# Attention in a two-layer hybrid model: K in one padded tile per head, and projection units taken as their buffers come free

## The chip, the cores and the metric

One core of a Trainium2 chip runs the whole inference step as one program. The metric is the device time of one execution in microseconds (us). The engines are TensorE (PE, with its weight loads shown as PEld), VectorE (DVE), ScalarE (ACT), GpSimd (POOL) and SyncE (SP, which issues DMA transfers). Each engine works through its own instructions in order.

## What is computed

The model has a state-space layer and an attention layer, each followed by a feed-forward layer; 1024 new prompt rows and 64 sample rows (continuing an older stream) are processed, 1088 in all, 1024 wide. The change is in the attention layer only. Cut to what matters:

```
K, V = split(rmsnorm(x) @ w_kv)                 # 16 heads of 64, K and V shared, also outputs
q    = rmsnorm(x) @ w_q
# prompt: queries in chunks of 64, each sees its own chunk and the 8 before
# sample: 64 queries see 512 cached keys and 64 new ones
s = q k^T * 64**-0.5 + rel_bias[clip(qpos - kpos, -256, 256) + 256]
s = where(valid, s, -inf);  p = softmax(s);  o = p v;  mixer = o @ w_o
```

## The kernel before

Projections run in three slices of columns (rows of x): `SL` = 0 to 383, 384 to 767, 768 to 1087; the last 64 columns of slice 2 are the sample. Heads are taken in eight pairs. For each pair and slice there is one projection **unit** for each of K, V and Q: nine units a pair. A unit is 24 matmuls (`mm`, lines 454 to 456: eight steps of depth, three passes that give float32 precision from split operands), 384 or 320 columns wide. It is issued in four parts of six matmuls, and between the parts TensorE takes other work from a list of tasks.

Attention of a pair runs in nine **blocks** of 128 queries; block 8 is the sample with 64. A block has three stages:

- **Scores.** For each head, K times the high and the low part of Q into a PSUM tile `S` (lines 1692 and 1693), then VectorE adds the bias and takes the extreme (1702), ScalarE takes the exponential (1707), and VectorE the reciprocal and the scaling (1708, 1709). A block sees up to five tiles of 128 keys, 640 columns.
- **Transposes.** TensorE transposes the probabilities (`ptp`, 1724), VectorE (first head) and ScalarE (second head) copy them out (1729, and 1731 for the last 64 rows of block 8).
- **Values.** Probabilities times V (`po`, 1763), three blocks at once when the first block of the next slice has had its transposes.

`S` and `ptp` share two PSUM buffers; the projections have two of their own. Each of K's tiles holds one slice of one head in `[high; low]` halves (`evk`, lines 1586 to 1603, with two ScalarE casts 1598 and two VectorE subtractions 1599), so that the scores of a block are cut wherever its keys cross a slice: block 6 needs three pieces of 128, 384 and 128 columns for each head. `evq` (1605 to 1625) does the same for Q with four casts; `evv` (1637) hands V to a task that transposes it (`vtp`, 1632, copied at 1634). `load_bias` brings each head's bias by DMA and has POOL clear its two corners (1578, 1579); there are three such buffers for two heads a pair. The weights of later units are prepared by ScalarE and VectorE (`hl`, lines 350 and 353).

The order on TensorE is written by the program: it runs a modelled clock `st.t` and picks tasks by it. The orders on the other engines are found by a scheduler with priorities when the program is built. The units of a pair come in a fixed order, K V Q of slice 0, then of slice 1, then of slice 2; before each the loop waits until the buffers it writes are free, and meanwhile other tasks run:

```
for s, i in [(s, i) for s in range(NSL) for i in range(3) if j > 1 or s == 2 or i == 2]:
    q = 3 * j + s
    if (s, i) == (2, 0):
        st.spawn(side_task(j))
    st.wait_for(lambda: cur["A"] >= 3 * (q - 1) if i == 2 else free_q(q, "AC"[i]))
    units(ws[i], j, evs[i], (s,))
```

`cur["A"]` counts the blocks whose scores are issued. `V`, `A`, `G` and `PE` stand for the four engines, `P` is 128, `T` 1088, `WIN` 640.

Of the kernel before, what the change touches and what calls it, by code (L numbers as in the profile page):

```python
# [374 lines left out]
def hybrid_kernel(  # L375
# [1165 lines left out]
    with ExitStack() as es:  # L1541
# [5 lines left out]
        pos = {}  # L1547

        def load_pair(j):
            kqv[j] = dict(K={}, Q={}, V={})  # L1550

        def load_side(j):
            d = kqv[j]
# [26 lines left out]
                bias.append(bt)  # L1580
            kqv[j]["bias"] = bias

        def k_tiles():
            return [sb2.tile([P, 384], F32R, tag=f"K{e}", bufs=KBUF, name=f"K{e}") for e in range(2)]

        def evk(j):
            d = kqv[j]

            def f(s, p_):
                n = SL[s][1]  # L1590
                st.wait_for(lambda: ("rb", s) in done)
                kf = sb2.tile([P, 384], F32, tag="kqv", bufs=2, name="kf")
                with tc.high_priority(HIP):
                    V.tensor_tensor(kf[:, :n], p_[:, :n], rba[s][:, :n], op=ALU.mult)
                Kd = d["K"].get(s) or k_tiles()
                for e in range(2):
# [3 lines left out]
                d["K"][s] = Kd  # L1600
                if s:
                    a_, b_, c_ = (128, 384, 0) if s == 1 else (0, 320, 256)
                    nc.sync.dma_start(kT_o[j * P:(j + 1) * P, c_:c_ + b_ - a_], kf[:, a_:b_])
            return f

        def evq(j):
            def f(s, p_):
                n = SL[s][1]

                Q = [[sb2.tile([P, 384], F32R, tag=f"Q{x}{e}", bufs=2, name=f"Q{x}{e}") for x in "hl"] for e in range(2)]  # L1610
                kqv[j]["Q"][s] = Q
                qf = sb2.tile([P, 384], F32, tag="kqv", bufs=2, name="qf")
                with tc.high_priority(HIP):
                    V.scalar_tensor_tensor(qf[:, :n], p_[:, :n], 0.125, rba[s][:, :n], op0=ALU.mult, op1=ALU.mult)
                for e in range(2):
                    qh, ql = Q[e]
                    A.copy(qh[H2[e], :n], qf[H2[e], :n])
# [9 lines left out]
        def v_task(j, s, vt):  # L1627
            Vn = kqv[j]["V"][s] = sb2.tile([P, 3, P], F32, tag="Vn", bufs=KBUF, name="Vn")
            pt = ax("vtp")
            for i in range(3):  # L1630
                L = CHL[3 * s + i]
                PE.transpose(pt[:L, i * P:(i + 1) * P], vt[:, i * P:i * P + L], ident)
            nf = 3 if s < 2 else 2
            V.tensor_copy(Vn[:, :nf, :], pt[:, :nf * P].rearrange("p (a b) -> p a b", b=P))
            if s == 2:
                V.tensor_copy(Vn[:64, 2, :], pt[:64, 256:384])
# [18 lines left out]
        def att_task(j, b):  # L1655
# [6 lines left out]
            )  # L1662
            L = CHL[b]

            pcs_ = []
# [11 lines left out]
            parts, bank, fill = [], 0, 0  # L1677
            for kd_, ko, fw in pcs_:
                if fill + fw > 512:
                    bank, fill = bank + 1, 0  # L1680
                parts.append((bank, fill, kd_, ko, fw))
                fill += fw
            split = sum(p_[4] for p_ in parts if p_[0] == 0)
            nkt = (w_ + P - 1) // P
            sts = []
            for e in range(2):
                sp = psS.tile([P, 2, 512], F32, tag="S", name="S")
                qs = slice(i * P, i * P + L)
                qh, ql = d["Q"][s][e]
                for bank, f0, kd_, ko, fw in parts:  # L1690
                    dst = sp[:L, bank, f0:f0 + fw]
                    PE.matmul(dst, qh[:, qs], kd_[e][:, ko:ko + fw], start=True, stop=False)
                    PE.matmul(dst, ql[:, qs], kd_[e][:, ko:ko + fw], start=False, stop=True)
# [3 lines left out]
                brev = bt[:L, 0:w_][:, ::-1] if b < 8 else bt[:L, 64:640][:, ::-1]  # L1697

                low = TOP
                with tc.high_priority(ATP):  # L1700
                    for pi, (f0, f1) in enumerate([(0, split)] + ([(split, w_)] if split < w_ else [])):
                        V.tensor_tensor_reduce(  # L1702
                            out=sc[:L, f0:f1], in0=sp[:L, pi, :f1 - f0], in1=brev[:, f0:f1],
                            scale=-1.0, scalar=low, op0=ALU.add, op1=ALU.min, accum_out=mx[:L, pi:pi + 1],
                        )
                        low = mx[:L, pi:pi + 1]
                    A.activation(sc[:L, :w_], sc[:L, :w_], AF.Exp, bias=low, scale=-1.0, accum_out=mx[:L, 3:4])
                    V.reciprocal(mx[:L, 3:4], mx[:L, 3:4])
                    V.tensor_scalar(sc[:L, :w_], sc[:L, :w_], mx[:L, 3:4], None, op0=ALU.mult)
# [9 lines left out]
            for e in range(2):  # L1719
                pT = late["sb3"].tile([P, 5, P], F32, tag="pT", bufs=6, name="pT")  # L1720
                pt = psS.tile([P, 2, 512], F32, tag="S", name="ptp").rearrange("p a b -> p (a b)")
                for kt in range(nkt):
                    kw = min(P, w_ - kt * P)
                    PE.transpose(pt[:kw, kt * P:kt * P + L], sts[e][:L, kt * P:kt * P + kw], ident[:L, :L])  # L1724
                ptv = pt[:, :640].rearrange("p (a b) -> p a b", b=P)
                nfull = w_ // P
                cpf = A.copy if e else V.tensor_copy
                with tc.high_priority(ATP):
                    cpf(pT[:, :nfull, :L], ptv[:, :nfull, :L])
                    if nfull < nkt:  # L1730
                        cpf(pT[:64, nfull, :L], ptv[:64, nfull, :L])
                PTs.append(pT)
            cur["B"] = seqn + 1
            cost += 1.1 * w_ / 640
# [10 lines left out]
        def values(blocks):  # L1745

            cost = 0
            while blocks:
# [3 lines left out]
                    pos["po"] = ax("po")  # L1752
                po = pos["po"]
                for kt in range(nkt):
                    kw = min(P, w_ - kt * P)
                    for e in range(2):
                        if 3 * s + i < 8:
                            vs = d["V"][(k0 + kt) // 3][:, (k0 + kt) % 3, 64 * e:64 * e + 64]
                        elif kt < 4:
                            vs = d["Cv"][:, kt, 64 * e:64 * e + 64]  # L1760
                        else:
                            vs = d["V"][2][:64, 2, 64 * e:64 * e + 64]
                        PE.matmul(  # L1763
                            po[64 * e:64 * e + 64, i * P:i * P + L], vs, PTs[e][:kw, kt, :L],
                            start=(kt == 0), stop=(kt == nkt - 1),
                        )
                if i == 2:
# [57 lines left out]
                if s and w is wv:  # L1825
                    W.put()

        kqv[0]["K"][2] = k_tiles()
        units(W.get(), 1, evk, (0, 1))
        W.put()  # L1830
        st.wait_for(lambda: 2 in done)
# [25 lines left out]
        for j in range(1, 8):  # L1857
# [3 lines left out]
            ws = [W.get(), W.get() if j > 1 else wv, W.get()]  # L1861
            evs = [evk, evv, evq]

            for s, i in [(s, i) for s in range(NSL) for i in range(3) if j > 1 or s == 2 or i == 2]:
                q = 3 * j + s
                if (s, i) == (2, 0):
                    st.spawn(side_task(j))
                st.wait_for(lambda: cur["A"] >= 3 * (q - 1) if i == 2 else free_q(q, "AC"[i]))
                units(ws[i], j, evs[i], (s,))
                if s == 2:  # L1870
                    W.put()
# [130 lines left out]
```

## Time and profile before

| | |
|---|---|
| time, median of 3 runs | 2980.72 us (2979.49 to 2980.98) |
| profiled execution, its own time | 2979.66 us |
| its span, first to last instruction | 2978.0 us |
| granted TensorE clock, mean | 0.996 of full speed |
| TensorE busy | 2921.0 us, 98% of the span |
| VectorE, ScalarE, POOL busy | 69%, 47%, 24% |
| attention stage | about 1643 to 2137 us of the span |
| a steady pair of heads | 62.77 to 63.57 us |

In a timeline row stand the start, the busy time, the engine and line, the operation with its output and inputs, the shape, and how many instructions are joined; in brackets the idle time in front of it and what ended that. Starts of joined or pipelined matmuls tell their pitch better than their busy times, which overlap.

### The profile page before, as it was taken

What the parts mean: (1) busy time and instruction counts of PE and PEld (TensorE: products, weight loads), DVE (VectorE), ACT (ScalarE), POOL (GpSimd) and SP (SyncE); (2) the same over time, 40 slices, a digit from 0 to 9 for tenths busy, and PEclk for the clock granted to TensorE, in tenths of its full rate; (3) what the DMA queues carried; (4) which work ended last, traced back from release to release, by engine and by line L of the source; (5) the groups of instructions that cost most, each with busy time, mean ns of one, the idle gap of its engine ahead of it and who ended that gap; (6) DMA issues with size and microseconds to landing.
All of it is one profiled execution on the core that took longest, in us unless ns stands there. A gap on an engine that the chain in (4) does not pass through costs nothing.

```text
span 2978.0 us, 56302 instructions
## 1 busy us (share of the span) xinstructions
PE 2921.0 (98%) x21626; PEld 2871.4 (96%) x21626; DVE 2040.2 (69%) x4471; ACT 1394.1 (47%) x2530; POOL 719.2 (24%) x821
## 2 busy tenths in 40 slices
PE   8999999999999999999999999999999999999999
PEld 7899999999999999999999899999999999999999
DVE  7887878885768545584567777777678645475544
ACT  6554646454453223344445665555653323244443
POOL 1333333331122343451111000000131343351111
PEclk9999999999999999999999999999999999999999
DMA  3333333244563222345665222223365222255654
GB/s 122 113 105 99 102 100 106 90 120 148 171 185 113 82 81 73 96 153 171 202 192 157 83 80 73 65 64 95 115 180 174 80 81 75 78 153 174 215 178 137
DMA packets 201551, 363.36 MB, mean 122 GB/s; under 512 B 20545, under 2 KB 149281, under 8 KB 201281
## 3 DMA queue, kind: packets, MB, share of 16 engines
q1 hardware_dynamic: 199488, 353.39, 38.6%
q0 software_dynamic: 1792, 6.36, 1.1%
q8 instruction: 170, 2.79, 0.4%
q14 instruction: 101, 0.82, 0.1%
HBM read 292.47 MB, written 62.74 MB: 119 GB/s over the span
## 4 chain that ended last, share of the span: by engine, by line
PE 83%; DVE 9%; DMA 3%; ACT 2%; issue 2%; POOL 0%; SPq 0%; DVEq 0%; ACTq 0%; POOLq 0%
PE px L1280 9%; PE px L1281 9%; PE px L1282 9%; PE mm L454 7%; PE mm L456 7%; PE mm L455 7%; PE po L1480 6%; PE po L1481 6%; PE po L1479 6%; PE mmx L455 3%; PE mmx L454 3%; PE mmx L456 3%; PE po L1763 2%; PE ptp L1724 1%; DVE sc L1702 1%
## 5 line engine op out<-in xcount | busy, mean ns | idle before, releaser
L454 PE MATMUL mm<-r,hl 128*128 128x384 f32 (+2 forms) x1664 | 555.2, 334 | 5.7 <-ACT BT L768 3.0
L456 PE MATMUL mm<-r,hl 128*128 128x384 f32 (+2 forms) x1664 | 539.0, 324 | 3.6 <-DVE hl L353 2.9
L455 PE MATMUL mm<-r,hl 128*128 128x384 f32 (+2 forms) x1664 | 537.8, 323 | 0.0
L341 DVE TENSOR_TENSOR hl<-raw,hl 128x1024 fp32r<-128x1024 f32 (+1 forms) x219 | 257.6, 1177 | 227.5 <-ACT hl L340 223.2
L1281 PE MATMUL px<-r,hl 128*128 128x288 f32 (+1 forms) x1184 | 347.3, 293 | 0.0
L454 PEld LDWEIGHTS mm<-r,hl 128*128 128x128 f32 x1664 | 314.7, 189 | 8.8 <-ACT BT L768 3.2
L456 PEld LDWEIGHTS mm<-r,hl 128*128 128x128 f32 x1664 | 313.9, 189 | 5.1 <-DVE hl L353 3.9
L455 PEld LDWEIGHTS mm<-r,hl 128*128 128x128 f32 x1664 | 315.0, 189 | 0.1
L1280 PE MATMUL px<-r,hl 128*128 128x288 f32 x1056 | 310.9, 294 | 0.0
L1282 PE MATMUL px<-r,hl 128*128 128x288 f32 x1056 | 310.7, 294 | 0.0
L340 ACT CAST hl<-raw 128x1024 fp32r<-128x1024 f32 (+1 forms) x219 | 219.9, 1005 | 176.1 <-PE po L1481 99.7
L480 POOL TENSOR_TENSOR ssum<-ssum,sq 128x256 f32<-128x256 f32 (+3 forms) x97 | 129.2, 1333 | 639.6 <-ACT sq L479 624.3
L1281 PEld LDWEIGHTS px<-r,hl 128*128 128x128 f32 x1184 | 222.3, 188 | 0.0
L1282 PE MATMUL px<-rx,hl 128*128 128x256 f32 x768 | 214.9, 280 | 6.6 <-DVE hl L341 6.6
L1280 PE MATMUL px<-rx,hl 128*128 128x256 f32 x768 | 215.4, 280 | 0.8 <-ACT hl L340 0.8
L1480 PE MATMUL po<-rx,hl 128*128 128x384 f32 (+1 forms) x624 | 201.5, 323 | 0.2 <-DVE rx L1344 0.2
L1280 PEld LDWEIGHTS px<-r,hl 128*128 128x128 f32 x1056 | 198.4, 188 | 0.2 <-DVE u L1295 0.2
L1282 PEld LDWEIGHTS px<-r,hl 128*128 128x128 f32 x1056 | 198.3, 188 | 0.0
L1479 PE MATMUL po<-rx,hl 128*128 128x384 f32 (+1 forms) x608 | 197.3, 324 | 0.0
L1481 PE MATMUL po<-rx,hl 128*128 128x384 f32 (+1 forms) x608 | 196.5, 323 | 0.0
L1281 PE MATMUL px<-rx,hl 128*128 128x256 f32 x640 | 178.7, 279 | 0.0
L290 POOL TENSOR_TENSOR tt<-raw 128x512 f32<-128x512 f32 x40 | 55.4, 1386 | 438.3 <-DMA raw<-in_w_f_dram 333.9
(359 smaller groups left out, 8052.6 us busy)
## 6 DMA issues: line engine op xcount, KB each, us to landing
raw<-in_w_f_dram SPq DMA_DIRECT2D x154, 512.0 KB, 3.8
rx<-in_w_f_dram SPq DMA_DIRECT2D x54, 512.0 KB, 3.7
raw<-in_w_in_dram SPq DMA_DIRECT2D x40, 512.0 KB, 3.6
MT<-ascr SPq DMA_DIRECT2D x48, 384.0 KB, 4.3
sg<-hscr SPq DMA_DIRECT2D x88, 192.0 KB, 3.5
raw<-in_w_f_dram SPq DMA_DIRECT2D x44, 384.0 KB, 3.4
raw<-in_w_so_dram SPq DMA_DIRECT2D x32, 512.0 KB, 4.0
raw<-in_w_kv_dram SPq DMA_DIRECT2D x18, 512.0 KB, 3.5
```

Source lines behind the costliest of these rows:

```text
L340: self.nc.scalar.copy(h, v)
L341: (eng or self.eng or self.nc.vector).tensor_tensor(lo, v, h, op=ALU.subtract)
L454: PE.matmul(ps[:, :n], h_, xh, start=(first and i == 0), stop=False)
L455: PE.matmul(ps[:, :n], h_, xl, start=False, stop=False)
L456: PE.matmul(ps[:, :n], l_, xh, start=False, stop=(last and i == nk - 1))
L480: (eng or G).tensor_tensor(ssum[:, :n], ssum[:, :n], q[:, :n], op=ALU.add)
L1280: PE.matmul(ps, wh, ah[:, k, :], start=(k == 0), stop=False)
L1281: PE.matmul(ps, wh, al[:, k, :], start=False, stop=False)
L1282: PE.matmul(ps, wl, ah[:, k, :], start=False, stop=(k == 3))
L1479: PE.matmul(ps[:, :n], wh, xh, start=(k == 0), stop=False)
L1480: PE.matmul(ps[:, :n], wh, xl, start=False, stop=False)
L1481: PE.matmul(ps[:, :n], wl, xh, start=False, stop=(k == FT - 1))
```

## The change

Five edits go together.

1. K is one tile per head and pair, 9 x 128 columns, in place of one per slice. Its last 64 columns (behind the sample's 64 keys) are set to zero by POOL, and so are the last 64 query columns of Q's slice 2 and of V's.
2. Scores are cut by width and no more by slice: up to 512 columns in one piece, 640 in two of 320.
3. Block 8 is computed like the others with 128 queries and 128 new keys, of which 64 are padding; its transposes are 128 x 128, and one copy takes what two did.
4. V's transposes are always full and copied at once.
5. The units of a pair are taken in the order in which their buffers come free: the first, of those not done yet, of K, of V or of Q that may go now.

```diff
-                Kd = d["K"].get(s) or k_tiles()
-                for e in range(2):
-                    A.copy(Kd[e][H2[e], :n], kf[H2[e], :n])
-                    V.tensor_tensor(Kd[e][H2[1 - e], :n], kf[H2[e], :n], Kd[e][H2[e], :n], op=ALU.subtract)
+                if not d["Kt"]:
+                    d["Kt"] = [sb2.tile([P, 9 * P], F32R, tag=f"K{e}", bufs=2, name=f"K{e}") for e in range(2)]
+                    for Kd in d["Kt"]:
+                        G.memset(Kd[:, T:].bitcast(F32), 0.0)
+                for e, Kd in enumerate(d["Kt"]):
+                    hi, lo = Kd[H2[e], 384 * s:384 * s + n], Kd[H2[1 - e], 384 * s:384 * s + n]
+                    A.copy(hi, kf[H2[e], :n])
+                    V.tensor_tensor(lo, kf[H2[e], :n], hi, op=ALU.subtract)
...
+                if s == 2:
+                    for q_ in Q[0] + Q[1]:
+                        G.memset(q_[:, n:].bitcast(F32), 0.0)
...
+                    G.memset(vt[:, n:], 0.0)
...
-                for t_ in range(3):
-                    c0, c1 = max(k0, 3 * t_), min(b + 1, 3 * t_ + 3)
-                    if c0 < c1:
-                        pcs_.append((d["K"][t_], (c0 - 3 * t_) * P, (c1 - c0) * P))
+                half = w_ if w_ <= 512 else w_ // 2
+                parts = [(c_ // half, d["Kt"], k0 * P + c_, half) for c_ in range(0, w_, half)]
             else:
-                k0 = 0
-                w_ = 576
-                pcs_ = [(d["Ck"], 0, 512), (d["K"][2], 256, 64)]
+                k0, w_, half = 0, WIN, 512
+                parts = [(0, d["Ck"], 0, 512), (1, d["Kt"], 8 * P, P)]
...
-                    PE.transpose(pt[:kw, kt * P:kt * P + L], sts[e][:L, kt * P:kt * P + kw], ident[:L, :L])
+                    PE.transpose(pt[:, kt * P:(kt + 1) * P], sts[e][:, kt * P:(kt + 1) * P], ident)
...
-            for s, i in [(s, i) for s in range(NSL) for i in range(3) if j > 1 or s == 2 or i == 2]:
+            def can(s, i):
                 q = 3 * j + s
+                return cur["A"] >= 3 * (q - 1) if i == 2 else free_q(q, "AC"[i])
+            left = [(s, i) for s in range(NSL) for i in range(3) if j > 1 or s == 2 or i == 2]
+            while left:
+                st.wait_for(lambda: any(can(*x) for x in left))
+                seen, now = set(), None
+                for x in left:
+                    if x[1] not in seen and can(*x):
+                        now = x
+                        break
+                    seen.add(x[1])
...
+                left.remove(now)
+                s, i = now
```

The units of a steady pair come out in another order, and with them the evacuations on the other engines. Three places show it.

TensorE in the first pair, from the end of block 6's scores (`S`, with its K, and Q high and low) over block 5's transposes (`ptp`) to block 7's scores and the values. Before:

```order
L1692 MATMUL S<-K_18759,Qh_19252 128x128
L1693 MATMUL S<-K_18759,Ql_19253 128x128
L1724 MATMUL ptp<-ident,sc 128x128 x10
L1692 MATMUL S<-K_18706,Qh_19250 128x384
L1693 MATMUL S<-K_18706,Ql_19251 128x384
L1692 MATMUL S<-K_18758,Qh_19250 128x256
L1693 MATMUL S<-K_18758,Ql_19251 128x256
```

After, the end of the 18 projection matmuls that now follow block 6's scores, the transposes, six more, and block 7's first pieces:

```order
L454 MATMUL mm<-r,hl 128x320
L455 MATMUL mm<-r,hl 128x320
L456 MATMUL mm<-r,hl 128x320
L1712 MATMUL ptp<-ident,sc 128x128 x10
L454 MATMUL mm<-r,hl 128x320
L455 MATMUL mm<-r,hl 128x320
L456 MATMUL mm<-r,hl 128x320
L454 MATMUL mm<-r,hl 128x320
L455 MATMUL mm<-r,hl 128x320
L456 MATMUL mm<-r,hl 128x320
L1681 MATMUL S<-K_18527,Qh_19244 128x320
L1682 MATMUL S<-K_18527,Ql_19245 128x320
```

Twenty-four matmuls of the next pair's K unit of slice 2 have moved here, from behind block 8.

TensorE in a steady pair, block 8's transposes, and the values of blocks 6 to 8 (`Vn` the new V, `Cv` the cached). Before, where twelve matmuls (the first and the last three are shown) stand between the two:

```order
L1724 MATMUL ptp<-ident,sc 128x64 x4
L1724 MATMUL ptp<-ident,sc 64x64
L454 MATMUL mm<-r,hl 128x320
L455 MATMUL mm<-r,hl 128x320
L456 MATMUL mm<-r,hl 128x320
...
L454 MATMUL mm<-r,hl 128x320
L455 MATMUL mm<-r,hl 128x320
L456 MATMUL mm<-r,hl 128x320
L1763 MATMUL po<-pT,Vn 64x128 x20
L1763 MATMUL po<-pT,Cv 64x64 x8
```

After:

```order
L455 MATMUL mm<-r,hl 128x384
L456 MATMUL mm<-r,hl 128x384
L1712 MATMUL ptp<-ident,sc 128x128 x10
L1747 MATMUL po<-pT,Vn 64x128 x20
L1747 MATMUL po<-pT,Cv 64x64 x8
L1747 MATMUL po<-pT,Vn 64x64 x2
L1712 MATMUL ptp<-ident,sc 128x128 x2
```

The twelve have gone to between block 7's transposes and block 8's scores. Before, block 8's transposes stood in the middle of K's unit of slice 2; now the matmuls right in front of them are the last of Q's unit of slice 1.

VectorE in a steady pair, from block 8's reductions on (the scores of both heads, then the next pair's block 0; `Vn` is V's copy, `kf` an evacuation of K). Before:

```order
L1708 RECIPROCAL mx<-mx 64x1
L1709 TENSOR_SCALAR sc<-sc,mx 64x576
L1708 RECIPROCAL mx<-mx 64x1
L1709 TENSOR_SCALAR sc<-sc,mx 64x576
L1702 ISA sc,mx<-S,bias 128x128
L1702 ISA mx 128x1
L1702 ISA sc,mx<-S,bias 128x128
L1702 ISA mx 128x1
```

After:

```order
L1698 TENSOR_SCALAR sc<-sc,mx 128x640
L1599 TENSOR_TENSOR K_20710<-kf,K_20710 64x320
L1691 ISA sc,mx<-S,bias 128x128
L1691 ISA mx 128x1
L1691 ISA sc,mx<-S,bias 128x128
L1691 ISA mx 128x1
L1697 RECIPROCAL mx<-mx 128x1
L353 SCALAR_TENSOR_TENSOR hl<-raw,pcs,hl 128x128
L1698 TENSOR_SCALAR sc<-sc,mx 128x640
```

The reciprocal and scaling of block 8's second head stand behind the next pair's block 0 now, with a weight preparation between them. On ScalarE the copy of block 8's transposes stands between the casts of the Q unit of slice 1:

```order
L1620 CAST Qh_21208<-qf 64x384
L1621 CAST Qh_21208<-qf 64x384
L1716 COPY pT<-ptp 128x5x64
L1620 CAST Qh_21210<-qf 64x384
L1621 CAST Qh_21210<-qf 64x384
```

Before, it stood behind all four casts, with K's casts of slice 2 after it.

More of the change, by code (lines that the diff above doesn't have):

```diff
@@ L1549, in load_pair @@
         def load_pair(j):
[L1550 removed]
+            kqv[j] = dict(K=set(), Kt=[], Q={}, V={})
         def load_side(j):
@@ L1630, in v_task @@
             for i in range(3):
[L1631 to L1636, printed above, removed]
+                PE.transpose(pt[:, i * P:(i + 1) * P], vt[:, i * P:(i + 1) * P], ident)
+            V.tensor_copy(Vn, pt[:, :3 * P].rearrange("p (a b) -> p a b", b=P))
             yield 0.33, 0
@@ L1696, in att_task @@
                 bt = d["bias"][e]
-                brev = bt[:L, 0:w_][:, ::-1] if b < 8 else bt[:L, 64:640][:, ::-1]
+                brev = bt[:, 0:w_][:, ::-1]
                 low = TOP
                 with tc.high_priority(ATP):
-                    for pi, (f0, f1) in enumerate([(0, split)] + ([(split, w_)] if split < w_ else [])):
+                    for pi, (f0, f1) in enumerate([(0, half)] + ([(half, w_)] if half < w_ else [])):
                         V.tensor_tensor_reduce(
-                            out=sc[:L, f0:f1], in0=sp[:L, pi, :f1 - f0], in1=brev[:, f0:f1],
-                            scale=-1.0, scalar=low, op0=ALU.add, op1=ALU.min, accum_out=mx[:L, pi:pi + 1],
-                        )
[L1706 to L1709, printed above, removed]
+                            out=sc[:, f0:f1], in0=sp[:, pi, :f1 - f0], in1=brev[:, f0:f1],
+                            scale=-1.0, scalar=low, op0=ALU.add, op1=ALU.min, accum_out=mx[:, pi:pi + 1],
+                        )
+                        low = mx[:, pi:pi + 1]
+                    A.activation(sc[:, :w_], sc[:, :w_], AF.Exp, bias=low, scale=-1.0, accum_out=mx[:, 3:4])
+                    V.reciprocal(mx[:, 3:4], mx[:, 3:4])
+                    V.tensor_scalar(sc[:, :w_], sc[:, :w_], mx[:, 3:4], None, op0=ALU.mult)
                 sts.append(sc)
@@ L1862, in hybrid_kernel @@
             evs = [evk, evv, evq]
-            for s, i in [(s, i) for s in range(NSL) for i in range(3) if j > 1 or s == 2 or i == 2]:
+            def can(s, i):
                 q = 3 * j + s
+                return cur["A"] >= 3 * (q - 1) if i == 2 else free_q(q, "AC"[i])
[8 more added lines that the diff above has]
+                    seen.add(x[1])
+                if now is None:
+                    now = left[0]
+                    st.wait_for(lambda: can(*now))
+                left.remove(now)
+                s, i = now
                 if (s, i) == (2, 0):
                     st.spawn(side_task(j))
-                st.wait_for(lambda: cur["A"] >= 3 * (q - 1) if i == 2 else free_q(q, "AC"[i]))
                 units(ws[i], j, evs[i], (s,))
```

32 lines of the change are left out of this document (8 added, 24 removed).

## The prediction

> **What bounds the kernel now.** I read the page first: the busy shares, then the chain that ended last.
>
> ```profile
> PE 2921.0 (98%) x21626; PEld 2871.4 (96%) x21626; DVE 2040.2 (69%) x4471; ACT 1394.1 (47%) x2530; POOL 719.2 (24%) x821
> PE 83%; DVE 9%; DMA 3%; ACT 2%; issue 2%; POOL 0%; SPq 0%; DVEq 0%; ACTq 0%; POOLq 0%
> ```
>
> TensorE is nearly always busy and most of the last chain. So a gain is either a TensorE idle removed or TensorE work that gets shorter, and both have to lie in the attention stage, the only one the diff touches. Next, the engines' busy time in five windows, each one steady pair of heads (columns: length; then busy and count of PE, PEld, DVE, ACT, POOL; granted clock, DMA share, GB/s).
>
> ```profile
> 1715.47:1779.04 63.57, 62.58 (x501) 59.49 (x501) 48.80 (x153) 36.89 (x93) 0.62 (x4) 1.00 0.23 68
> ...
> sum 315.94, PE 311.71 PEld 297.21 DVE 243.69 ACT 185.66 POOL 3.04; mean PE 62.34 PEld 59.44 DVE 48.74 ACT 37.13 POOL 0.61
> ```
>
> A steady pair lasts 63.2 us (315.94 / 5), and PE is idle 4.23 / 5 = 0.85 us of it. That is small, and the clock is full, so there is no throttling to win back. The waits of the attention stage say what the idle is (total us, times, longest):
>
> ```profile
> POOL bias L1578 <- DMA bias<-in_rbrow_dram: 437.6, 14, 62.2
> ...
> PEld S L1692 <- DVE pT L1729: 9.3, 19, 0.7
> ...
> DVE sc L1702 <- POOL bias L1578: 6.9, 7, 1.3
> ...
> PE ptp L1724 <- DVE mx L1702: 4.9, 9, 1.9
> ```
>
> Scores wait for a PSUM buffer that the copies of the transposes hold (9.3 us), transposes for one that the reductions of the scores hold (4.9 us). Both share two buffers. POOL's 437.6 us harm only where VectorE then waits for POOL, 6.9 us.
>
> **The first pair (part a).** Its PE timeline, from block 6's scores on:
>
> ```profile
> 1683.22 0.22 PE L1692 MATMUL S<-K,Qh 128*128 128x128 f32 x1
> ...
> 1686.84 0.74 PE L1724 MATMUL ptp<-ident,sc 128*128 128x128 f32 x5 [1.92 <-DVE mx L1702]
> 1687.85 1.12 PE L1724 MATMUL ptp<-ident,sc 128*128 128x128 f32 x5 [0.27 <-DVE mx L1702]
> 1688.68 0.69 PE L1692 MATMUL S<-K,Qh 128*128 128x384 f32 x1
> ...
> 1691.12 3.43 PE L1763 MATMUL po<-pT,Vn 128*64 128x128 f32 x56
> ...
> 1697.84 0.45 PE L1692 MATMUL S<-Ck,Qh 128*64 128x512 f32 x1 [0.37 <-DVE pT L1729]
> ...
> 1706.46 0.82 PE L1724 MATMUL ptp<-ident,sc 64*128 64x64 f32 x10
> 1707.21 0.42 PE L454 MATMUL mm<-r,hl 128*128 128x320 f32 x1
> ...
> 1708.28 2.40 PE L1763 MATMUL po<-pT,Vn 128*64 128x128 f32 x40
> ...
> 1711.34 0.44 PE L1724 MATMUL ptp<-ident,sc 128*128 128x128 f32 x2
> ...
> 1711.77 0.31 PE L455 MATMUL mm<-r,hl 128*128 128x320 f32 x1
> ...
> 1712.94 0.31 PE L454 MATMUL mm<-r,hl 128*128 128x320 f32 x1
> ```
>
> From block 6's scores to the next pair's block 0 transposes it is 1711.34 - 1683.22 = 28.12 us. Nothing stands between block 6's scores and block 5's transposes, so these wait for the reductions. Now 18 projection matmuls of 320 columns stand there and 6 more behind the transposes; they are taken from behind block 8, so the work in the stretch is the same. The pitch of a 320-column matmul is (1712.94 - 1711.77) / 8 = 0.146 us.
>
> The stretch, put together anew: block 6's scores 8 x 0.146 = 1.17; 18 matmuls 2.63, and 0.1 lost at a start; block 5's transposes 1.1; 6 matmuls 1.0; block 7's scores 1.17; from its end to block 8's scores as now, 1697.84 - 1691.12 = 6.72. The rest needs rows of a steady pair:
>
> ```profile
> 1741.53 0.22 PE L1692 MATMUL S<-K,Qh 128*128 128x128 f32 x1
> ...
> 1743.07 0.39 PE L454 MATMUL mm<-r,hl 128*128 128x384 f32 x1
> ...
> 1745.21 0.71 PE L1724 MATMUL ptp<-ident,sc 128*128 128x128 f32 x5
> 1746.16 0.74 PE L1724 MATMUL ptp<-ident,sc 128*128 128x128 f32 x5 [0.24 <-DVE mx L1702]
> 1746.65 0.42 PE L454 MATMUL mm<-r,hl 128*128 128x384 f32 x1
> ...
> 1758.64 1.25 PE L1724 MATMUL ptp<-ident,sc 128*128 128x128 f32 x10
> 1760.27 0.45 PE L1692 MATMUL S<-Ck,Qh 128*64 128x512 f32 x1 [0.37 <-DVE pT L1729]
> ...
> 1761.63 0.55 PE L1632 MATMUL vtp<-ident,vt 128*128 128x128 f32 x3
> ```
>
> Five transposes take 1746.65 - 1746.16 = 0.49, twelve 384-column matmuls 1745.21 - 1743.07 = 2.14, block 8's scores 1761.63 - 1760.27 = 1.36. So behind 1697.84: scores 1.36, 2 x 12 matmuls 4.3, block 0's scores about 0.4 (4 pieces at 0.1, estimated), block 8's transposes 1.1, values 1711.34 - 1708.28 = 3.06, and a new wait of 0.45 (below): 10.7. With the 13.9 ahead it is 24.6, against 28.12: **-3.5 us**.
>
> **Each of the six steady pairs (part b).** All of it on PE.
> 1. Block 6's scores are 8 matmuls in place of 12: 1743.07 - 1741.53 = 1.54 becomes 1.17, **-0.36**. Block 3's go from 8 to 4 of 512 columns, **-0.15** by the same pieces, half as many.
> 2. Block 5's transposes wait between their two heads: 1746.16 - 1745.21 = 0.95 for the first five, 0.49 for the next. VectorE tells why:
>
> ```profile
> 1741.73 0.56 DVE L1614 SCALAR_TENSOR_TENSOR qf<-mm,rbf 128x384 f32<-128x384 f32 x1 [1.37 <-PE mm L456]
> ...
> 1743.34 0.68 DVE L1702 CUSTOM_DVE_ANT_0 sc<-S,bias 128x512 f32<-128x512 f32 x1
> ```
>
> The unit before ended right at block 6's scores, and its evacuation (1741.73) holds the reductions back until 1743.34. Now six matmuls stand ahead of block 5's scores, so the unit that is evacuated here ends six matmuls (1.05 us) sooner. The reductions start about 1 us sooner, the transposes 0.36 sooner: **-0.44**, with hardly any margin.
>
> 3. The same six matmuls stand between block 3's transposes and V's transposes and block 5's scores, which follow each other directly now: **-0.3**, estimated as one wait of the 0.5 that the 19 score waits average (9.3 / 19) less a start.
> 4. Twelve matmuls stand between block 7's transposes and block 8's scores. Before: 1760.27 - 1758.64 - 2 x 0.49 = 0.65 lost. Against it 0.1 for one more start and 0.2 for block 8's wider pieces: **-0.3**.
> 5. Block 8's transposes are as wide as all others: ten in about 1.0 to 1.1 against 0.75 (1707.21 - 1706.46): **+0.3**.
> 6. Before, 12 matmuls lie between block 8's transposes and the values. Now none: the copies of the transposes have only blocks 6 and 7 of the values (about 2.4 us, row 1708.28) to hide behind. The copy on ACT stands behind the casts of a Q unit, which ends only where block 8's transposes begin, and behind five weight casts. Rows of the same place two pairs on:
>
> ```profile
> 1823.93 0.45 PE L1692 MATMUL S<-Ck,Qh 128*64 128x512 f32 x1 [0.37 <-DVE pT L1729]
> ...
> 1824.74 0.68 DVE L1702 CUSTOM_DVE_ANT_0 sc<-S,bias 64x512 f32<-64x512 f32 x1 [0.86 <-PE S L1693]
> ...
> 1829.95 0.29 DVE L1702 CUSTOM_DVE_ANT_0 sc<-S,bias 128x128 f32<-128x128 f32 x1 [1.03 <-POOL bias L1578]
> ...
> 1832.13 0.51 ACT L1617 CAST Qh<-qf 64x384 fp32r<-64x384 f32 x1 [1.02 <-DVE qf L1614]
> ...
> 1834.16 0.36 ACT L1729 COPY pT<-ptp 128x256 f32<-128x256 f32 x1
> L350 ACT ACTIVATE hl<-raw,pcs 128x128 fp32r<-128x128 f32 x176 | 57.2, 391 | 5.2 <-PE mm L456 4.2 <-DMA raw<-in_w_kv_dram 0.3
> ```
>
> From the start of block 8's scores: the reduction of the next pair's block 0 comes at 1829.95 - 1823.93 = 6.0; an exponential behind it (about the length of a weight cast, estimated) to 7.2; five weight casts of 0.39 to 9.2; two casts of 0.51 to 10.2; the copy, wider than the 0.36 shown, and the way to PE, to 11.1 (estimated). PE is at block 8's values at 1.4 (scores) + 0.4 (V's transposes) + 1.9 (six matmuls of each width) + 0.4 (block 0's scores) + 3.1 (18 matmuls at 2.14 / 12, less a start) + 1.1 + 2.4 = 10.7. **+0.4 to 0.5**, taken as 0.45, between 0 (the weight casts come earlier, as ACT is half idle) and 1.3 (they come late and the copy waits for both Q heads).
>
> The sum: -0.36 - 0.15 - 0.44 - 0.3 - 0.3 + 0.3 + 0.45 = **-0.8 us a pair**, -4.8 for six. It fits in the 0.85 idle plus the half us of pieces.
>
> **What costs nothing.** POOL's clears of the padded tails wait behind POOL's wait for the bias, but nobody needs them before that bias has come. Block 8's reduction takes as long for 128 rows as for 64: 0.68 us for 512 columns at 1743.34 and at 1824.74. The last pair has no next units to move and nets **+0.1** (re-cut against wider block 8). Later stages keep their order.
>
> All: -3.5 - 4.8 + 0.1 = **-8.2 us**. The profiled execution took 2979.66 us, 1.06 below the median of 2980.72, so its differences carry over to the median as they are: **2972.5 us**.
>
> The trace's rows for the re-cut of block 6 are 1.54 us for twelve matmuls. [...]
>
> **The rivals.**
> *The wait moves (0.20).* The copy of block 8's transposes is late by 1.3 to 2 us a pair, since no matmuls cover it. For it: the ACT queue above, where the copy's place is the worst of all engines. Against: ACT is busy 37.13 of 63.2 us, it can be ahead with the weight casts. Seven pairs x (1.3 to 2 less 0.45) = +6 to +11 on -8.2: 2978.5 to 2983.5, no change.
>
> *Slower: VectorE is held by the bias (0.12).* On VectorE the reciprocal and scaling of block 8's second head now stand behind the reduction of the next pair's block 0, which waits for POOL and so for a DMA:
>
> ```profile
> 1762.79 3.61 DMA bias<-in_rbrow_dram
> ```
>
> Its buffer is freed by block 8's own first head, then 3.61 us of transfer. Block 8's transposes wait for that scaling. Reduction at 6.0, done 0.3 later, reciprocal and scaling to about 7.1; the second head's transposes are due at 1.4 + 0.4 + 1.9 + 0.4 + 3.1 + 0.5 = 7.7. The margin is 0.6 us. It decides where the bias comes 0.6 + 8.2 / 7 = 1.8 us later than now; at 4 us later the cost is 7 x 3.4 = +24 on -8.2, 2996 us. Against: the transfer has the same length in the pairs and starts no later. [...]
>
> *Nothing comes of it (0.08).* PE is 98% busy, and each wait that goes shows up at the next shared buffer: 2978 to 2982. Against: the first pair's 1.92 us has a plain cover now.
>
> **How the numbers follow.** My forecast has 0.60: 2972.5, itself 2968 (no wait at 6, 3.2 us less, and part of the estimates) to 2978. The range goes to 2982 to take in most of the moved wait and of "nothing": about 0.15 lies above, few below 2967. Under 0.2% (6 us) this kernel's change cannot be told from none: faster means below 2974.8, slower above 2986.7. Of the forecast's 0.60 some 0.08 lies above 2974.8, and the rest with a few of the other cases' lower ends makes 0.58 faster; same 0.28 (the moved wait, nothing, and the forecast's upper end); slower 0.14 (the bias, and the moved wait grown beyond its bound).
>
> **What would show it.** In the changed profile: block 5's transposes in the first pair without the 1.92 us wait (step a); block 6's scores in 1.2 us; no wait at block 8's scores; a wait of values for the ACT or DVE copies of block 8, below 0.6 us for my forecast, over 1.3 for the moved wait; no transposes of block 8 waiting for L1698. A pair's period of 62.4 us says I am right, 63.2 says nothing came, over 64 the bias. I am wrong, too, if the time changes outside the attention stage.

## The result, and the profile after

The changed kernel takes 2971.70 us (median of 7 runs, 2968.48 to 2974.23) against 2981.54 us of the kernel before (7 runs, 2979.49 to 2983.44): ratio 0.9968, 95% interval 0.9958 to 0.9977, 9.8 us less. The forecast was 2972.5, by 8.2 us less. The same kernel, run again later beside its experiments, gave 2968.39 us and 0.9959 (0.9946 to 0.9971), so a median of a few runs moves by 3 us. The kernel before, run in each group of experiments, gave medians of 2980.50, 2981.20 and 2981.33. The finer readings below come from the profiles of the attention stage, where two profiles of the changed kernel differ by 0.45 us in six pairs.

Six steady pairs, each window from one pair's block 0 transposes to the next's (columns as in the prediction; the `sum` row of before ahead, then two rows and the sum of after):

```profile
sum 379.17, PE 373.84 PEld 356.66 DVE 294.81 ACT 225.64 POOL 3.33; mean PE 62.31 PEld 59.44 DVE 49.13 ACT 37.61 POOL 0.56
```

```profile
1710.18:1771.60 61.42, 61.35 (x495) 59.58 (x492) 47.91 (x152) 36.90 (x93) 1.67 (x11) 1.00 0.21 66
1771.60:1833.17 61.57, 61.46 (x493) 59.60 (x492) 48.06 (x152) 37.11 (x93) 1.67 (x11) 1.00 0.25 74
...
sum 369.05, PE 368.55 PEld 357.33 DVE 289.98 ACT 222.91 POOL 9.59; mean PE 61.42 PEld 59.55 DVE 48.33 ACT 37.15 POOL 1.60
```

Six pairs lost 10.12 us, 1.69 a pair. TensorE's idle in them went from 5.33 us (379.17 - 373.84) to 0.50 us, which is 4.83 of it; the other 5.29 is busy time (373.84 to 368.55). Some of that is fewer pieces. Some is waiting: the busy time of a matmul runs past the start of the next one (0.31 us against a pitch of 0.15), so short waits hide in it. So the stretches below are read from start to start. The waits of the attention stage after the change:

```profile
POOL K L1595 <- PE S L1682: 270.7, 12, 45.2
...
DVE sc L1691 <- POOL bias L1578: 4.3, 7, 0.7
PE S L1681 <- DVE pT L1716: 2.9, 5, 0.9
PE ptp L1712 <- DVE mx L1691: 0.9, 1, 0.9
```

POOL now waits 270.7 us to clear K's tail, and nobody waits for that. Transposes that waited 4.9 us for reductions wait 0.9, once, in the last pair. The five waits of scores for VectorE's copies lie in the first and the last pair too, none in the six between. The rows of the first pair, which answer to those from 1683.22 on before:

```profile
1685.05 0.31 PE L1681 MATMUL S<-K,Qh 128*128 128x320 f32 x1
...
1686.22 0.31 PE L454 MATMUL mm<-r,hl 128*128 128x320 f32 x1
...
1688.85 1.25 PE L1712 MATMUL ptp<-ident,sc 128*128 128x128 f32 x10
1689.86 0.39 PE L454 MATMUL mm<-r,hl 128*128 128x320 f32 x1
...
1691.42 0.42 PE L1681 MATMUL S<-K,Qh 128*128 128x320 f32 x1 [0.44 <-DVE pT L1716]
...
1698.13 1.31 PE L1712 MATMUL ptp<-ident,sc 128*128 128x128 f32 x10 [0.81 <-DVE pT L1716]
1700.00 0.47 PE L1681 MATMUL S<-Ck,Qh 128*128 128x512 f32 x1 [0.56 <-DVE pT L1716]
...
1707.26 2.40 PE L1747 MATMUL po<-pT,Vn 128*64 128x128 f32 x40
```

Block 6's scores take 1686.22 - 1685.05 = 1.17 us, and block 5's transposes wait for nothing. But the copies behind them are late now: 0.44 us at block 7's scores, 0.81 at block 7's transposes and 0.56 at block 8's scores, where 0.37 stood before. The values of blocks 6 to 8 take 1710.18 - 1707.26 = 2.92 us here.

In a steady pair, block 6's scores and block 5's transposes, then block 8's transposes and its values:

```profile
1740.86 0.31 PE L1681 MATMUL S<-K,Qh 128*128 128x320 f32 x1
...
1744.15 1.25 PE L1712 MATMUL ptp<-ident,sc 128*128 128x128 f32 x10
...
1767.11 1.25 PE L1712 MATMUL ptp<-ident,sc 128*128 128x128 f32 x10
1768.29 2.40 PE L1747 MATMUL po<-pT,Vn 128*64 128x128 f32 x40
1770.53 0.96 PE L1747 MATMUL po<-pT,Cv 128*64 128x64 f32 x15
...
1771.60 0.44 PE L1712 MATMUL ptp<-ident,sc 128*128 128x128 f32 x2
```

Block 8's transposes take 1768.29 - 1767.11 = 1.18 us, and the values 1771.60 - 1768.29 = 3.31 (also the mean of the six pairs; 3.24 in the second profile) against 3.06 before (1711.34 - 1708.28), so 0.25 us longer. The wait in them is more than that, 0.39 us, since padded values that wait for nothing take 2.92, as in the first pair. The padding itself shortens them: block 8's last twenty matmuls took 0.83 us before (1773.41 to 1774.24), with 64 keys in the last four, and take 0.69 in the first pair (1709.49 to 1710.18). The wait ends with ScalarE's copy of block 8's transposes, behind two casts of Q:

```profile
1769.86 0.51 ACT L1621 CAST Qh<-qf 64x384 fp32r<-64x384 f32 x1
1770.39 0.43 ACT L1716 COPY pT<-ptp 128x320 f32<-128x320 f32 x1
```

### The profile page after: what moved, and what is told of

The parts are those of the page before. It is cut to its first block, busy times and chain, and to the rows that moved or that the text cites. A ratio compares the mean times of both kernels' runs of the same rounds, so it can differ in the third digit from the quotient of the medians.

```text
span 2969.1 us, 56218 instructions
## 1 busy us (share of the span) xinstructions
PE 2916.9 (98%) x21562; PEld 2871.9 (97%) x21562; DVE 2037.2 (69%) x4455; ACT 1394.6 (47%) x2522; POOL 723.7 (24%) x877
## 4 chain that ended last, share of the span: by engine, by line
PE 85%; DVE 8%; DMA 3%; ACT 2%; issue 2%; POOL 0%; SPq 0%; DVEq 0%; ACTq 0%; POOLq 0%
PE px L1280 9%; PE px L1281 9%; PE px L1282 9%; PE mm L454 7%; PE mm L456 7%; PE mm L455 7%; PE po L1480 6%; PE po L1481 6%; PE po L1479 6%; PE mmx L455 3%; PE mmx L454 3%; PE mmx L456 3%; PE ptp L1712 2%; PE po L1747 2%; PE yp L816 1%
```

## The experiments

**The order alone.** The new loop over units in the old kernel, in which a block's cost in the modelled clock is rounded up for block 8, so that TensorE's order is that of the changed kernel:

```diff
+            def can(s, i):
+                return cur["A"] >= 3 * (q - 1) if i == 2 else free_q(q, "AC"[i])
...
-            cur["t"] = st.t + 1.1 * w_ / 640 + GAP_A
+            cur["t"] = st.t + 1.1 * (640 if w_ == 576 else w_) / 640 + GAP_A
```

> The kernel before with the new order of units alone: K's tiles, the cuts of the scores and block 8 stay as they were. The order on TensorE is that of the changed kernel, with the old pieces. Theory (the order removes waits, re-cut and padding cancel each other): the first pair 3.0 us shorter, each of six steady pairs 1.7 us shorter, and 2 us given back in the last pair, where VectorE is behind: 11 us faster than before, 1 to 2 us faster than the changed kernel. Rival (the gain is half order, half re-cut, as in the prediction's sum): 7 us faster than before. Rival (the waits only move): no faster than before.

2970.37 us (5 runs), ratio 0.9965 (0.9953 to 0.9978): 10.1 us less than before. The six pairs:

```profile
sum 370.54, PE 369.12 PEld 356.12 DVE 291.23 ACT 223.10 POOL 3.20; mean PE 61.52 PEld 59.35 DVE 48.54 ACT 37.18 POOL 0.53
```

8.6 us less in six pairs, 1.44 each, where 1.7 was expected. The order alone brings most of the gain, so it does not just move its waits. It was expected to beat the changed kernel and did not: its six pairs are 1.5 to 1.9 us longer, and its median lies between the two of the changed kernel.

**The tiles, cuts and padding alone**: the changed kernel with the old loop.

```diff
-            left = [(s, i) for s in range(NSL) for i in range(3) if j > 1 or s == 2 or i == 2]
-            while left:
...
+            for s, i in [(s, i) for s in range(NSL) for i in range(3) if j > 1 or s == 2 or i == 2]:
```

> The changed kernel with the old fixed order of units: one padded tile of K, new cuts, block 8 with 128 queries. Theory: the re-cut takes 0.53 us a pair off, the padding adds 0.43 at block 8's transposes and 0.14 at its scores, so no change from before, within 1 us either way. Rival (the cut is a good part of the gain): 4 us faster. In the profile block 6's scores take 1.17 us in place of 1.53, and block 5's transposes still wait for the reductions.

2973.83 us (8 runs), 0.9975 (0.9965 to 0.9986): 6.7 us less than before. My theory, that re-cut and padding cancel, falls.

```profile
sum 373.86, PE 369.67 PEld 356.46 DVE 294.44 ACT 226.35 POOL 10.20; mean PE 61.61 PEld 59.41 DVE 49.07 ACT 37.72 POOL 1.70
```

Six pairs are 5.3 us shorter. The two halves add up to 8.6 + 5.3 = 13.9, and together they bring 10.1. Of the 3.8 us of overlap, 3.0 is one wait that each removes by itself: block 5's transposes take 1.52 us before (mean of the six) and 1.01 or 1.02 with either half or both. The rest is a balance of places that come out otherwise with both halves than the two would add up to: the values 1.4 us longer and block 8's transposes 1.0, block 1's scores 2.0 shorter. VectorE and TensorE in this kernel, at block 6's scores:

```profile
1742.82 0.56 DVE L1617 SCALAR_TENSOR_TENSOR qf<-mm,rbf 128x384 f32<-128x384 f32 x1 [1.38 <-PE mm L456]
1743.40 0.49 DVE L1691 CUSTOM_DVE_ANT_0 sc<-S,bias 128x320 f32<-128x320 f32 x1
...
1744.82 0.55 DVE L1622 TENSOR_TENSOR Ql<-qf,Qh 64x384 fp32r<-64x384 f32 x1
```

```profile
1745.91 1.25 PE L1712 MATMUL ptp<-ident,sc 128*128 128x128 f32 x10
```

The evacuation of Q still ends right here, as in the old order, but three of the four reductions run ahead of Q's low part (1743.40 against 1744.82). In the kernel before, one subtraction stood ahead of all of them, up to 1743.34, and the other ahead of the second:

```profile
1742.87 0.55 DVE L1619 TENSOR_TENSOR Ql<-qf,Qh 64x384 fp32r<-64x384 f32 x1 [0.58 <-ACT Qh L1617]
...
1744.06 0.56 DVE L1619 TENSOR_TENSOR Ql<-qf,Qh 64x384 fp32r<-64x384 f32 x1
```

So block 5's transposes wait no more, though no unit has moved. Why the build put them first was not tried apart: the scores end 0.36 us sooner and come in even halves.

**The cut alone undone**: the changed kernel with the old boundaries of pieces, out of the one tile.

```diff
-                parts = [(c_ // half, d["Kt"], k0 * P + c_, half) for c_ in range(0, w_, half)]
+                for t_ in range(3):
+                    c0, c1 = max(k0, 3 * t_), min(b + 1, 3 * t_ + 3)
+                    if c0 < c1:
...
+                        parts.append((bank, d["Kt"], c0 * P, fw_, fill))
```

> The changed kernel with the scores cut where slices of 384 end, as before (128, 384, 128 for block 6; 384 and 128 for block 3), out of the one tile of K. All else stays as changed. Theory (the trace's rows): 0.36 us a pair more for block 6 and 0.17 for block 3, times eight: 4.2 us slower than the changed kernel. Rival (the time of a matmul is its columns, pieces cost nothing): no change from the changed kernel.

2973.57 us (11 runs), 0.9976 (0.9967 to 0.9985), 1.9 us over the changed kernel by the medians, 5.2 over its second set of runs. In the profile:

```profile
1740.27 0.22 PE L1691 MATMUL S<-K,Qh 128*128 128x128 f32 x1
...
1741.69 0.27 PE L1692 MATMUL S<-K,Ql 128*128 128x128 f32 x1
1743.95 1.25 PE L1722 MATMUL ptp<-ident,sc 128*128 128x128 f32 x10
```

Block 6's last piece starts 1.42 us after its first; in the changed kernel the whole block takes 1.17. The six pairs sum to 371.70 us by the starts of block 0's transposes, +2.65, 0.44 a pair. So pieces cost, near what the rows of before said (0.51), and the "no change" of a time by columns falls. The scores alone are 0.57 us a pair longer; the values' wait is 0.18 shorter in return. Block 5's transposes wait for nothing here either, with the new order and the old cut.

**Block 8's transposes with 64 queries.**

```diff
-                    PE.transpose(pt[:, kt * P:(kt + 1) * P], sts[e][:, kt * P:(kt + 1) * P], ident)
+                    PE.transpose(pt[:, kt * P:kt * P + L], sts[e][:L, kt * P:(kt + 1) * P], ident[:L, :L])
```

> The changed kernel, but block 8's transposes take only the 64 real queries (the padded scores and softmax stay). Theory (the copy on ScalarE behind Q's casts sets when block 8's values can go, not the transposes): most of the 0.43 us a pair turns up as a longer wait at block 8's values, and the gain over the changed kernel is about 1 us in all. Rival (the transposes' own width is on the path): 0.43 x 8 = 3.4 us faster than the changed kernel.

2966.30 us (5 runs), 0.9949 (0.9936 to 0.9963). The six pairs come to 368.36 us, 0.7 or 0.2 less than the two profiles of the changed kernel, and not the 0.43 x 6 = 2.6 of the transposes. The wait that came in its place is at block 1's scores:

```profile
1770.33 0.44 PE L1712 MATMUL ptp<-ident,sc 128*128 128x128 f32 x2
1772.66 0.39 PE L1681 MATMUL S<-K,Qh 128*128 128x256 f32 x1
```

```profile
1771.06 1.26 ACT L1562 CAST Ck<-cr 64x512 fp32r<-64x512 f32 x2
1772.34 0.27 ACT L1716 COPY pT<-ptp 128x128 f32<-128x128 f32 x1
```

The two transposes of block 0 are ready by about 1770.8 and lie until 1772.34, because ScalarE's casts of the sample's cached keys stand ahead of its copy; the wait ends with that copy. VectorE's copy of the other head is as late (1772.43), behind the other half of the same split. The theory foresaw a gain of about 1 us, and that fits, but it looked for the wait at the values, where it shows in two of the six pairs alone; the medians say 5.4 us against the first set of runs and 2.1 against the second, too far apart to read.

**Two bias buffers in place of three**, which doubles the wait of the slower rival.

```diff
-                bt = late["sb3"].tile([P, WIN], F32, tag="bias", bufs=3, name="bias")
+                bt = late["sb3"].tile([P, WIN], F32, tag="bias", bufs=2, name="bias")
```

> The changed kernel with two bias buffers in place of three, so both heads' bias for the next pair are loaded only when block 8 has used its own. This doubles the suspected wait of VectorE. Theory (the margin behind block 8's second head was about 0.6 us): the reduction of the next pair's block 0 comes some 1.5 to 2 us later, the second head's scaling is late for its transposes by about 1 us a pair: 5 to 8 us slower than the changed kernel. Rival (the bias has a wide margin): no change. Rival (the prediction's slower case with its full price): over 12 us slower.

2974.31 us (11 runs), 0.9979 (0.9970 to 0.9988): 5.9 us slower than the changed kernel run beside it.

```profile
1765.46 0.71 PE L1712 MATMUL ptp<-ident,sc 128*128 128x128 f32 x5
1767.00 0.77 PE L1712 MATMUL ptp<-ident,sc 128*128 128x128 f32 x5 [0.83 <-DVE mx L1691]
```

```profile
1764.52 0.55 DVE L1698 TENSOR_SCALAR sc<-sc,mx 128x640 f32<-128x640 f32 x1
...
1766.65 0.29 DVE L1691 CUSTOM_DVE_ANT_0 sc<-S,bias 128x128 f32<-128x128 f32 x1 [0.16 <-POOL bias L1578]
```

The size was as expected and the path was not. Block 8's transposes take 2.30 us on average, 1.1 more; the values lose their wait of 0.39 in return, and the six pairs are 3.9 us longer than in the changed kernel's first profile. The second head's scaling (1764.52) is in time, since the build placed it ahead of the reduction that waits. What waits is the second head's transposes, for the PSUM buffer that block 0's scores hold until that reduction has run (1766.65).

**The cached keys split later**: after block 2's scores of the next pair. TensorE's order is the same.

```diff
-            yield 0, 0, lambda: cur["C"] >= 9 * j
+            yield 0, 0, lambda: cur["C"] >= 9 * j and cur["A"] >= 9 * j + 3
```

> The changed kernel, with the sample's cached keys of the next pair loaded and split after its block 2's scores rather than right behind block 8's values. TensorE's order is the same. Theory (on ScalarE and VectorE the split of the cached keys stands in front of the copies of block 0's transposes, and block 1's scores wait for these): 0.1 us a pair less at block 1's scores, and most of the 1.9 us of waiting in the last pair gone; the wait at block 8's values stays. About 2 us faster than the changed kernel. Rival (the copies are late for other reasons): no change.

2998.87 us (5 runs), 1.0062 (1.0050 to 1.0075): 17.7 us slower than before, 30.5 slower than the changed kernel beside it. Six pairs take 393.27 us, 4 us a pair more:

```profile
1721.87 0.39 PE L1682 MATMUL S<-K,Ql 128*128 128x512 f32 x1
1726.09 0.55 PE L1712 MATMUL ptp<-ident,sc 128*128 128x128 f32 x3 [1.75 <-DVE mx L1691]
1728.00 0.90 PE L1712 MATMUL ptp<-ident,sc 128*128 128x128 f32 x3 [1.37 <-DVE mx L1691]
```

```profile
1724.50 0.69 DVE L1563 TENSOR_TENSOR Ck<-cr,Ck 64x512 fp32r<-64x512 f32 x1 [0.66 <-ACT Ck L1562]
1725.33 0.69 DVE L1691 CUSTOM_DVE_ANT_0 sc<-S,bias 128x512 f32<-128x512 f32 x1
```

Block 3's scores are there at 1722.3, and their reduction starts at 1725.33, right behind the split. Block 2's transposes (the rows on TensorE) wait for it. The raw cached keys are loaded into two of the four `sc` buffers that the reductions write. That these lie free behind block 8 and not at block 3 is inferred; that the buffers are the reason is shown two experiments on.

**Both edits together.**

> Both: block 8's transposes take 64 queries, and the cached keys are split later. With narrow transposes alone a pair got back 0.35 us at block 1's scores, so theory: both together keep the whole 0.43 of the transposes and the 0.15 to 0.25 of the values' wait, 0.6 to 0.7 us a pair against the changed kernel, 4 to 6 us in all with the last pair. Rival (another wait takes the place): no more than the 1 us of the narrow transposes alone.

2999.36 us (5 runs), 1.0059 (1.0047 to 1.0072). The six pairs take 395.82 us and wait at the same place.

**The late split with two buffers of its own**, without and with the narrow transposes:

```diff
-                cr = late["sb3"].tile([P, WIN], F32, tag="sc", bufs=4, name="cr")[:, :PAST]
+                cr = late["sb3"].tile([P, PAST], F32, tag="cr", bufs=2, name="cr")
```

> As the run with the cached keys split later, but they are loaded into two buffers of their own, not into two of the four that hold scores and probabilities. Theory (in that run block 3's reductions waited for these buffers): the 4 us a pair are gone, and what was expected there comes: block 1's scores wait no more, the last pair loses its 1.9 us, about 2 us faster than the changed kernel. Rival (the split itself, 2.6 us of ScalarE and VectorE at block 3, is in the way wherever it goes): still 1 us a pair or more slower than the changed kernel.

> The same with block 8's transposes at 64 queries. Theory: 0.6 to 0.7 us a pair shorter than the changed kernel's 61.5 us, 4 to 6 us faster than it in all, 14 to 16 us faster than before. Rival (VectorE is behind in any case around block 8): a pair of 61.4 us, 1 us faster than the changed kernel.

Without: 2970.16 us (5 runs), 0.9966 (0.9954 to 0.9979). The 4 us a pair are gone, so the `sc` buffers were the reason. But a pair is no shorter than the changed kernel's (368.70 us for six against 369.05 and 368.60): the values lose 0.39 us of waiting, from 3.31 to 2.92, and block 0's scores of the next pair gain 0.43. The 2 us that were expected did not come.

With: 2965.79 us (5 runs, 2965.42 to 2966.75), 0.9948 (0.9935 to 0.9962), the lowest median of all, 15.5 us less than before. Narrow transposes without the late split gave 2966.30 (2965.56 to 2969.16), so by the times the two can't be told apart; by the six pairs this one is 1.6 us shorter.

```profile
1761.28 0.69 DVE L1563 TENSOR_TENSOR Ck<-cr,Ck 64x512 fp32r<-64x512 f32 x1
...
1763.49 0.33 DVE L1691 CUSTOM_DVE_ANT_0 sc<-S,bias,mx 128x128 f32<-128x128 f32 x1
```

```profile
1763.88 0.33 PE L1681 MATMUL S<-K,Qh 128*128 128x128 f32 x1 [0.23 <-DVE mx L1691]
```

```profile
sum 366.79, PE 365.13 PEld 353.84 DVE 289.36 ACT 221.64 POOL 9.96; mean PE 60.86 PEld 58.97 DVE 48.23 ACT 36.94 POOL 1.66
```

Six pairs are 1.8 to 2.3 us shorter than the changed kernel's, about half of what theory gave; the rest is the wait at block 0's scores (0.43 a pair). With the loads free to start early, the build put part of the split ahead of the last three of block 8's four reductions (1761.28), and block 0's scores wait for the last of them (1763.49).

**The changed kernel again.**

> The changed kernel once more, on the same chip as these three, so that differences of 1 to 5 us can be read. Theory: about 9 us faster than before, with six steady pairs of 61.5 us and the last pair's waits of 1.9 us as in its first profile.

2968.39 us (5 runs), 0.9959 (0.9946 to 0.9971); its six pairs take 368.60 us.

## Why the prediction was right

The sign, the places and the total were right: 8.2 us forecast, 9.8 and 12.8 measured in two sets. That the total came so close is in part luck, since its terms were off in opposite directions: six steady pairs gave 10.1 us and not 4.8, the first pair 3.0 and not 3.5, and the last pair took back 2 us where 0.1 stood.

- **First pair, -3.5:** from block 6's scores to the next pair's block 0 transposes it is 1710.18 - 1685.05 = 25.1 us against 28.1, so -3.0. The wait of block 5's transposes went as told. The copies that now run late (0.44, 0.81 and 0.56 in the rows above) had been taken as they were: up to block 8's scores it is 15.0 us and not 13.9. Behind them it is 10.2 and not 10.7, since the wait of 0.45 at the values isn't there in this pair.
- **A steady pair, -0.8, measured -1.69.** By starts, means of the six pairs:

| place | forecast | measured |
|---|---|---|
| block 6's scores, 1.53 to 1.17 | -0.36 | -0.36 |
| block 3's scores, 1.09 to 0.92 | -0.15 | -0.17 |
| block 5's transposes, 1.52 to 1.01 | -0.44 | -0.51 |
| V's transposes and block 5's scores, less the start of the matmuls between | -0.3 | -0.32 |
| block 7's transposes and block 8's scores, 2.84 to 2.33, less the same | -0.3 | -0.41 |
| block 8's transposes, 0.75 to 1.18 | +0.3 | +0.43 |
| values, 3.06 to 3.31 | +0.45 | +0.25 |
| start of the matmuls that no longer stand ahead of the values | 0 | -0.19 |
| block 1's scores and the wait ahead of them | 0 | -0.20 |
| other places, each under 0.1 | 0 | -0.2 |

  At block 5's transposes the step's reason was half the story: it is a wait that either the order or the cut removes, as the two half changes showed.
- **The terms that were mis-sized** lie around the values. The wait itself was well foreseen, 0.39 against 0.45: ScalarE's copy ends 11.0 us behind the start of block 8's scores (1770.82 - 1759.84; the prediction has 11.1), and TensorE is at block 8's values after 10.7 (1770.53 - 1759.84; the prediction has 10.7):

```profile
1759.84 0.39 PE L1681 MATMUL S<-Ck,Qh 128*128 128x512 f32 x1
```

  What the sum put at nothing is that padded values take 0.14 less (2.92 against 3.06), and that a start of 0.19 is saved where the matmuls left; 0.17 of that comes back as the start of the values right behind block 8's transposes, which take 1.18 there and 1.01 in the old order with the same padding.
- **What was not foreseen in a pair:** block 1's scores waited in the kernel before in three of six pairs (0.60, 0.33 and 0.63 us over the pitch). After, nothing waits ahead of them, and 0.1 us is left inside them in five of the six: -0.20 on average.
- **Idle as the ceiling.** The prediction took the 0.85 us of idle and half a us of pieces for what a pair could gain, and a period of 62.4 us for the sign of being right. The pair gained 1.69 and takes 61.5: the idle of the profile isn't the sum of the waits. In the changed kernel a pair's idle is 0.08 us (0.50 / 6), while its values wait 0.39.
- **Outside the attention stage** nothing changed that can be told from scatter. Behind its last values it is 842.1 us before and 842.4 in both profiles after. Ahead of it, the first scores (the 11,622nd matmul in each profile) start at 1643.63 before, 1644.99 and 1643.23 after.
- **The last pair, +0.1, measured about +2:** the term that was wrong by most of its size. From block 0's transposes to the last values it takes 45.4 us before, 47.5 and 47.9 after. Rows of TensorE and VectorE in the changed kernel:

```profile
2082.36 0.38 PE L1681 MATMUL S<-K,Qh 128*128 128x256 f32 x1 [0.95 <-DVE pT L1716]
...
2083.32 0.38 PE L1681 MATMUL S<-K,Qh 128*128 128x256 f32 x1 [0.46 <-ACT pT L1716]
```

```profile
2081.15 0.96 DVE L1784 TENSOR_TENSOR r<-r 128x768 fp32r<-128x768 f32 x1 [0.85 <-ACT r L1783]
2082.02 0.28 DVE L1716 COPY pT<-ptp 128x128 f32<-128x128 f32 x1
```

  VectorE's copy of block 0's transposes stands behind the split of the output projection's input (`r`, the attention outputs of earlier pairs), which waits for ScalarE; ScalarE's copy, which ends the second wait, stands behind its casts of the cached keys (the second one from 2082.36, 0.62 us; the copy from 2083.00). The prediction looked for such copies in the steady pairs alone. In the second profile of the changed kernel the part behind the six pairs is as long (890.3 us against 887.5 before), and with the late split in its own buffers it is 888.8.
- **The rivals.** The moved wait is there with 0.39 us (0.33 in the second profile), not 1.3. The slower case did not happen. On VectorE of the changed kernel the reduction that waits for the bias, and the scaling of block 8's second head:

```profile
1765.46 0.29 DVE L1691 CUSTOM_DVE_ANT_0 sc<-S,bias 128x128 f32<-128x128 f32 x1 [0.58 <-POOL bias L1578]
...
1765.67 0.16 DVE L1697 RECIPROCAL mx<-mx 128x1 f32<-128x1 f32 x1
...
1766.00 0.55 DVE L1698 TENSOR_SCALAR sc<-sc,mx 128x640 f32<-128x640 f32 x1
```

  ScalarE was done with block 8's second head at 1764.84 (1764.65 + 0.19):

```profile
1764.65 0.19 ACT L1696 ACTIVATION_READ_ACCUMULATOR sc<-sc,mx 128x1 f32 x1
```

  Its reciprocal stands behind the waiting reduction all the same and starts at 1765.67, 0.83 us later, so VectorE took them in order here. The scaling ends at 1766.6, 1.1 us ahead of the second head's transposes (half of 1.18 us behind 1767.11). The experiment with two buffers showed that a later bias does cost time, and that it would come through the PSUM buffer first. "Nothing comes of it" is refuted by the pairs, 379.17 to 369.05 us for six.
- **The piece price.** The trace's 1.54 to 1.17 us was confirmed: block 6's scores take 1.17 in every kernel with the new cut and 1.53 in the two experiments with the old one. Undoing the cut cost 2.65 us in six pairs.

## What to carry to other kernels

Where one engine is 98% busy, a wait can still have two causes, each of which is enough to keep it or to remove it: undo each half of a change by itself before giving a gain to one, and don't add up the halves. A step that is freed on the critical engine shows what is late next on the helper behind it, here copies on VectorE and ScalarE behind splits that were not urgent; look for these in the odd stretches too, the first and the last pair. And before moving a load, look at whose buffer it borrows: 4 us a pair came from two borrowed buffers, and went when the load had its own.

## What the runs showed that I had not expected

A 384-column matmul right behind a 128-column one was followed after 0.22 to 0.23 us (starts 1743.07 and 1743.30 in the timeline before, 1740.44 and 1740.66 with the old cut) and not 0.17, as behind one of 384 columns (1743.30 to 1743.47), and the second of two 128-column matmuls after 0.11 and not 0.06 (1741.59 to 1741.70, against 1741.53 to 1741.59). So three pieces of 640 columns cost 0.18 us a head more than two even halves (1.53 less 1.17 us, for two heads).

The medians of the same kernel in two sets lay 3.3 us apart, while the six pairs of its two profiles agreed to 0.45 us. The two profiled executions themselves differ by 0.8 us (2970.80 and 2970.02), so they don't show where the 3.3 comes from. But the profiles do show scatter of that size ahead of the changed stage: the first scores start between 1642.0 and 1646.2 us in the twelve profiles, in which the same number of matmuls stands ahead of them, and at the 1000th matmul the starts already lie between 169.3 and 172.4. A change of a few us is better read inside its stage than from the total.
